# Gate and up products with the weights as the standing operand

## The chip, the cores and the metric

The kernel runs on one core of one Trainium2 chip. The metric is the device time of one execution in microseconds (us), the median of three runs. Below, PE is TensorE's matmul, PEld its loading of the standing operand ("weight load"), DVE is VectorE, ACT is ScalarE, POOL is GpSimd, SP is the engine that issues most DMAs. A matmul holds one operand still in the array (128 rows by up to 128 columns, loaded by an instruction of its own, LDWEIGHTS) and lets the other pass, up to 512 columns; the result goes to PSUM, which has 8 banks of 512 fp32 numbers per partition.

## The reference, cut to what matters

2048 tokens of width 1024 go through a mixing layer and then a mixture of experts: 32 experts of hidden width 512, every token to two of them. The part that the change touches, for the tokens `xblk` of expert `e`:

```python
hdn = jax.nn.silu(xblk @ w_gate[e]) * (xblk @ w_up[e])   # (tokens, 1024) @ (1024, 512), twice
return hdn @ w_down[e]                                    # (tokens, 512) @ (512, 1024)
```

The result is weighted by the router's share and added to the token's row. All is fp32.

## The kernel before

The first 1550 us or so (norm, projections, retention, RWKV, output product, routing) are not touched. Then comes the expert loop, and a final norm.

Products are made in the fp32r format, with each operand split into a high part (rounded by ACT) and a low part (the rest, subtracted by DVE). One product is then three passes into the same PSUM bank: high x high, low x high, high x low. `split_ps` (L171) makes such a pair from a PSUM bank.

The experts are put in an order by load: those at even places (`more(e)`, L43) get 128 + 64 rows of tokens, those at odd places 128. The loop runs over 96 stages (`stages`, L918): (e, 0) gate, (e, 1) up, (e, 2) down, in the order (e, 0), (e, 1), (e-1, 2), so that the down product of one expert comes after the up product of the next. A stage takes four weight chunks of 128 x 1024. They are loaded by SP eight chunks ahead and split by `splits` (L931) on ACT and DVE; six chunks are split before the loop starts. ACT, DVE, PE and POOL run the loop in the order in which it is written.

In a gate or up stage (`mms`, L1061) a 128 x 128 block of the turned tokens `xT` stands and 512 weight columns pass: 8 chunks of the contraction x 3 passes = 24. The result has tokens on partitions. The 64 further rows of an even expert are done by `mms64` and `pair` (L1044, L1081), one stage late in `rest` (L1158): high and low part of the 64 rows stand side by side as 128 columns, so 16 passes of 512 columns do; the two halves of the result are then added by `rows64` (L1090). `gate` applies SiLU, `hidden` multiplies (L1101, L1110).

The down product contracts over the hidden width, so the hidden tile has to have that on partitions: `hidden_turn` (L1121) transposes it on PE, four blocks of 128 x 128 (L1125) or four of 64 rows (`turn64`, L1033), into PSUM, and splits it from there. The tokens themselves are fetched by POOL (`gather`, L1012) and turned by PE in `turn` (L1018, the 128 rows, in the up stage of the expert before) and `turn1` (L1037, the 64 rows, after the second half of the down stage before it).

PSUM: three rotating banks `accr`, three `AL` for the 64-row results, two `tp` for transposes.

Of the kernel before, what the change touches and what calls it, by code (L numbers as in the profile page):

```python
# [9 lines left out]
F32 = mybir.dt.float32  # L10
# [122 lines left out]
def build(tc, A, out, dbg=None, phases=3):  # L133
# [562 lines left out]
    if True:  # L696
# [189 lines left out]
        hlp = lp("hlp", HB)  # L886
        xbp, hdp, htp, yop, xtp, tmp = gp("xbp", 1), gp("hdp", 1), gp("htp", 2), gp("yop", 2), gp("xtp", 2), gp("tmp", TB)
        xbs = [xbp.tile([128 - 64 * i, D], F32, name=f"xb{i}") for i in range(2)]
        hd1 = xbp.tile([64, 512], F32, name="hd1")
        for t in (*xbs, hd1):  # L890
            GP.memset(t, 0.0)

        RAW, LD, LAST, EX = [], [], [], {}
# [123 lines left out]

        def turn(e, hf):  # L1018
            if hf == 0:
                XT[0, e] = xtp.tile([128, 2, 8, 128], F32R, name="xT0", bufs=2)  # L1020
            xT = XT[0, e]
            ps = tp().rearrange("p (k t) -> p k t", k=4)
            hs = slice(hf * 4, hf * 4 + 4)
            for k in range(4):
                PE.transpose(ps[:, k], xbs[0][:, (hf * 4 + k) * 128:(hf * 4 + k + 1) * 128], ident)  # L1025
            split_ps(ps, xT[:, 0, hs], xT[:, 1, hs])

        def turn64(src, n, nm, pool, **kw):

            xT = pool.tile([128, n, 128], F32R, name=nm, **kw)  # L1030
            ps = tp().rearrange("p (k t) -> p k t", t=64)[:, 0:n]
            for k in range(n):
                PE.transpose(ps[:, k], src[:, k * 128:(k + 1) * 128], ident[0:64, 0:64])  # L1033
            split_ps(ps, xT[:, :, 0:64], xT[:, :, 64:128])
            return xT

        def turn1(e):  # L1037
            XT[1, e] = turn64(xbs[1], 8, "xT1", xtp, bufs=1)
            if more(e + 2):
                gather(1, e + 2)  # L1040

# [10 lines left out]
                if k:  # L1052
                    mm(ps, lhs[:, k], wa, False, k == nk - 1)

        def w_in(hl, k):
            return (hl[k // 2][:, z, (k % 2) * 512:(k % 2 + 1) * 512] for z in range(2))

        def w_dn(n):
            return lambda hl, k: (hl[k][:, z, n * 512:(n + 1) * 512] for z in range(2))

        def mms(st, hl, pss, half):  # L1061

            e, w = st
            n = 4 if w < 2 else 2
            for k in range(half * n, half * n + n):
                first, last = k == 0, k == 2 * n - 1
                if w < 2:
                    wa, wb = w_in(hl, k)
                    xT = XT[0, e]
                    mm(pss[0], xT[:, 0, k], wa, first, False)  # L1070
                    mm(pss[0], xT[:, 1, k], wa, False, False)
                    mm(pss[0], xT[:, 0, k], wb, False, last)
                else:
                    hT = HT[2 * e]
                    for n_ in range(2):
                        wa, wb = w_dn(n_)(hl, k)
                        mm(pss[n_], hT[:, 0, k], wa, first, False)
                        mm(pss[n_], hT[:, 1, k], wa, False, False)
                        mm(pss[n_], hT[:, 0, k], wb, False, last)

        def mms64(st, hl, pss):  # L1081

            e, w = st
            if w < 2:
                pair(pss[0], XT[1, e], hl, w_in, 8)
            else:
                for n in range(2):
                    pair(pss[n], HT[2 * e + 1], hl, w_dn(n), 4)

        def rows64(ps, dst, w=None):  # L1090
            t = tmp.tile([64, 512], F32, name="lo64")
            SC.copy(t, ps[64:128])
            if w is None:
                V.tensor_tensor(dst, ps[0:64], t, op=ALU.add)
            else:
                V.tensor_tensor(t, ps[0:64], t, op=ALU.add)
                SC.activation(dst, t, AF.Copy, scale=w)

        GT = {}

        def gate(e, b):  # L1101
            pg = PS.pop((2 * e + b, 0))[0]
            if b == 0:
                GT[e] = hdp.tile([128, 512], F32, name="hd0")
                SC.activation(GT[e], pg, AF.Silu)
            else:
                rows64(pg, hd1)
                SC.activation(hd1, hd1, AF.Silu)

        def hidden(e, b):  # L1110
            pu = PS.pop((2 * e + b, 1))[0]
            if b == 0:
                hd = GT.pop(e)
                V.tensor_tensor(hd, hd, pu, op=ALU.mult)
                HD.append((2 * e, hd))
            else:
                up = tmp.tile([64, 512], F32, name="up")
                rows64(pu, up)
                V.tensor_tensor(hd1, hd1, up, op=ALU.mult)

        def hidden_turn(i, hd):  # L1121
            if i % 2 == 0:
                ps = tp().rearrange("p (k t) -> p k t", k=4)
                for k in range(4):
                    PE.transpose(ps[:, k], hd[:, k * 128:(k + 1) * 128], ident)  # L1125
                HT[i] = htp.tile([128, 2, 4, 128], F32R, name="hT0")
                split_ps(ps, HT[i][:, 0], HT[i][:, 1])
            else:
                HT[i] = turn64(hd, 4, "hT1", htp)

        def result(e, b):
            pn = PS.pop((2 * e + b, 2))
            yo = yop.tile([64 if b else 128, D], F32, name=f"yo{b}", bufs=YB[b])
            for n in range(2):
                o, w = yo[:, n * 512:(n + 1) * 512], ws[b][:, e:e + 1]
                if b:
                    rows64(pn[n], o, w)
                else:
                    SC.activation(o, pn[n], AF.Copy, scale=w)  # L1139
            HT.pop(2 * e + b)  # L1140
            return yo
# [16 lines left out]
        def rest(st, hl):  # L1158

            e, w = st  # L1160
            if not more(e):
                return
            pz_ = PS[2 * e + 1, w]
            mms64(st, hl, pz_)
            r = (gate, hidden, result)[w](e, 1)
            if w == 1:
                HD.append((2 * e + 1, hd1))
            if w == 2:
                ADD.append((SI[0] + ADL[1], 1, e, r))

        mk("moe")
        g0 = gather(0, 0)
# [10 lines left out]
        with tc.manual_schedule(engines=MS):  # L1183
# [4 lines left out]
            for si, st in enumerate(stages):  # L1188
                SI[0] = si
                e, w = st  # L1190
                if si:
                    evict(stages[si - 1])
                if si == len(stages) - 4:
                    gfb = k2.tile([128, D], F32, name="gfb", tag="g2b")
                    SC.dma_start(gfb, A["gf"].broadcast_to([128, D]))
                hl = CH.pop(si)
                nps = 2 if w == 2 else 1
                PS[(2 * e, w)] = [accr.tile([128, 512], F32, name="acc") for _ in range(nps)]
                if more(e):
                    PS[(2 * e + 1, w)] = [AL[(na + i) % 3] for i in range(nps)]  # L1200
                    na += nps
                n0, n1, n2 = NSP[w]
                n0 += si < NXS
                splits(min(n0, SB))
                if si:
                    rest(stages[si - 1], HLP)
                HLP = hl
                splits(n0 - min(n0, SB))
                adds(si)
                for half in range(2):  # L1210
                    mms(st, hl, PS[(2 * e, w)], half)
                    if w == 1 and e + 1 < 32:
                        turn(e + 1, half)
                    elif w == 2 and half and more(e + 2):
                        turn1(e + 2)
                    elif HD and (w == 0 or si == len(stages) - 2):
                        hidden_turn(*HD.pop(0))
                    splits(n1 if half == 0 else n2)
                if w == 1 and e + 2 < 32:
                    gather(0, e + 2)  # L1220
# [7 lines left out]
        with tc.If(nov > 0):  # L1228
            with tc.For_i(0, 32, 1) as e:
                nb = nc.values_load(cni[0:1, 0, bass.ds(e, 1)], min_val=0, max_val=15)  # L1230
                s0 = nc.values_load(cni[0:1, 1, bass.ds(e, 1)], min_val=0, max_val=31 * TS + 192)
                with tc.For_i(0, nb, 1) as j:
                    tc_ = s2.tile([128, 2], F32, name="tc_")
                    for z, d in enumerate((tab_d, tw_d)):
# [4 lines left out]
                    GP.indirect_dma_start(out=xb, out_offset=None, in_=xt_d,  # L1239
                                          in_offset=bass.IndirectOffsetOnAxis(ap=to, axis=0),  # L1240
                                          bounds_check=S - 1, oob_is_err=False)
                    xT = xtp.tile([128, 8, 128], F32, name="xT1", bufs=1)
                    for hf in range(2):
                        ps = tp().rearrange("p (k t) -> p k t", k=4)
                        for k in range(4):
# [2 lines left out]
                    pgu = [accr.tile([128, 512], F32, name="acc") for _ in range(2)]  # L1248
                    for m, wn in enumerate(("wg", "wu")):
                        for k in range(8):  # L1250
                            w = xtp.tile([128, 2, 8, 128], F32, name="xT0").rearrange("p z k t -> p (z k t)")[:, 0:512]
                            SY.dma_start(w, A[wn][bass.ds(e, 1), k // 2, :, (k % 2) * 512:(k % 2 + 1) * 512]
                                         .rearrange("o p c -> (o p) c"))
                            mm(pgu[m], xT[:, k], w, k == 0, k == 7)
                    hd = hdp.tile([128, 512], F32, name="hd0")
                    SC.activation(hd, pgu[0], AF.Silu)
                    V.tensor_tensor(hd, hd, pgu[1], op=ALU.mult)
                    ps = tp().rearrange("p (k t) -> p k t", k=4)
# [3 lines left out]
                    V.tensor_copy(hT, ps)  # L1262
                    py_ = AL[0:2]
                    for k in range(4):
                        w = xtp.tile([128, 2, 8, 128], F32, name="xT0").rearrange("p z k t -> p (z k t)")[:, 0:D]
                        SY.dma_start(w, A["wd"][bass.ds(e, 1), k].rearrange("o p c -> (o p) c"))
                        for n in range(2):
                            mm(py_[n], hT[:, k], w[:, n * 512:(n + 1) * 512], k == 0, k == 3)
# [72 lines left out]
```

## Time and profile before

| | us |
|---|---|
| median of 3 runs (2396.13 to 2401.98) | 2398.52 |
| the profiled execution | 2402.56 |
| its span, first to last instruction | 2400.8 |
| PE busy in the span | 2196.5 |
| expert loop, first to last weight load on PE | about 1560 to 2344 |

In the profile a line such as "L152 PE MATMUL acc<-hl,xT 128\*128 128x512" is a matmul from line 152 (the helper `mm`) into the tile `acc`, with `hl` passing and `xT` standing, 128 rows by 128 columns of the standing operand, and 512 columns passing. The profile calls both fp32 and fp32r operands of matmuls f32. A plain fp32 matmul leaves two records, an fp32r one leaves one. Ends of matmuls are modelled; starts are recorded.

### The profile page before, as it was taken

To read this page: it belongs to the slowest core of one execution; us is meant where nothing else is said; L and a number is where in the kernel's file an instruction comes from. 1 tells how busy PE (TensorE), PEld (TensorE's weight loads), DVE (VectorE), ACT (ScalarE), POOL (GpSimd) and SP (SyncE) were. 2 spreads that over 40 slices of the span, in tenths; PEclk is the share of its full clock that TensorE was granted. 3 is DMA by queue.
4 is the path that set the end of the run, shared out by engine and by line. 5 is a ranking of instruction groups with operands and counts; after the bars stand their busy time and mean duration, and the time that the engine had idled before them with its cause. 6 is when DMAs were issued, how large, how long until landed. Compare 5 with 4: busy or idle time off the path is not lost. (4 is left out here: it accounts for less than half of the span.)

```text
span 2400.8 us, 36373 instructions
## 1 busy us (share of the span) xinstructions
PE 2196.5 (91%) x11816; PEld 1803.3 (75%) x11817; DVE 1698.5 (71%) x3594; ACT 1157.2 (48%) x1963; POOL 779.1 (32%) x1405
## 2 busy tenths in 40 slices
PE   5999889998998989999879999599999999999990
PEld 4887678887777877788768888577777777777770
DVE  4477775878766787667775665767777777777775
ACT  4353443434434344343332232267777677776763
POOL 2036444354531575146541433411112111111110
PEclk9999899999999999999969999799999999999995
DMA  6643254433544325433234445289999999999978
GB/s 212 211 148 99 82 172 135 135 94 99 173 142 122 98 88 167 125 101 99 84 96 130 127 163 175 94 304 306 307 321 299 304 300 320 310 293 303 310 233 297
DMA packets 291298, 454.78 MB, mean 189 GB/s; under 512 B 93392, under 2 KB 164496, under 8 KB 291088
## 3 DMA queue, kind: packets, MB, share of 16 engines
q1 hardware_dynamic: 277136, 414.10, 51.7%
q0 software_dynamic: 13824, 37.80, 7.0%
q8 instruction: 94, 1.54, 0.3%
q14 instruction: 100, 0.82, 0.1%
q10 hardware_dynamic: 144, 0.52, 0.1%
HBM read 375.18 MB, written 81.85 MB: 190 GB/s over the span
## 5 line engine op out<-in xcount | busy, mean ns | idle before, releaser
L152 PE MATMUL pj<-nT,whl 128*128 128x512 f32 x2496 | 628.1, 403 | 9.2 <-DVE nT L319 5.2
L152 PEld LDWEIGHTS pj<-nT,whl 128*128 128x128 f32 x2496 | 466.3, 192 | 107.0 <-DVE nT L319 5.7
L914 DVE TENSOR_TENSOR hl<-raw,hl 128x1024 fp32r<-128x1024 f32 x384 | 448.5, 1219 | 121.5 <-ACT hl L913 121.5
L152 PE MATMUL acc<-hl,xT 128*128 128x512 f32 (+1 forms) x2048 | 508.1, 400 | 0.0
L152 PEld LDWEIGHTS acc<-hl,xT 128*128 128x128 f32 (+1 forms) x2048 | 365.0, 182 | 100.0 <-ACT xT L172 0.2
L913 ACT CAST hl<-raw 128x1024 fp32r<-128x1024 f32 x384 | 378.4, 1048 | 6.7 <-PE tp L152 3.0
L249 ACT CAST whl<-wraw 128x512 fp32r<-128x512 f32 x248 | 152.5, 618 | 299.3 <-PE pj L152 236.1
L250 DVE TENSOR_TENSOR whl<-wraw,whl 128x512 fp32r<-128x512 f32 x248 | 188.0, 761 | 144.2 <-ACT whl L249 138.1
L152 PE MATMUL acc<-hl,hT 128*128 128x512 f32 (+1 forms) x1024 | 249.5, 398 | 0.0
L152 PEld LDWEIGHTS acc<-hl,hT 128*128 128x128 f32 (+1 forms) x1024 | 183.1, 181 | 51.8
L486 POOL TENSOR_TENSOR tm<-xl,ln 128x60 f32<-128x60 f32 (+24 forms) x496 | 173.8, 350 | 105.2 <-DMA ln<-nl_d 60.4
L488 POOL TENSOR_TENSOR xl<-xl,tm 128x60 f32<-128x60 f32 (+24 forms) x496 | 195.3, 394 | 36.6
L152 PE MATMUL acc<-wo,mT 128*128 128x512 f32 x768 | 192.3, 402 | 0.0
L1147 POOL DMA_INDIRECT h_d<-yo,ti x48 | 80.1, 1670 | 299.3 <-ACT yo L1139 180.1
L1014 POOL DMA_INDIRECT xb<-xt_d,ti x48 | 49.5, 1031 | 369.6 <-PE tp L1025 288.0
L152 PEld LDWEIGHTS acc<-wo,mT 128*128 128x128 f32 x768 | 142.3, 191 | 28.7 <-DVE mT L169 0.2
L152 PE MATMUL pj<-whl,nT 128*128 128x256 f32 x768 | 114.3, 298 | 0.3 <-DVE gs L600 0.2
L464 DVE TENSOR_TENSOR pt<-pb,cst 64x512 f32<-64x512 f32 x128 | 88.0, 687 | 22.6 <-PE pb L152 20.8
L152 PEld LDWEIGHTS pj<-whl,nT 128*128 128x128 f32 x768 | 101.6, 199 | 3.0 <-DVE gs L600 0.5
L499 POOL COPY mbd<-pt 32x128 f32<-32x128 f32 x64 | 20.7, 323 | 222.9 <-DVE pt L464 199.1
L172 ACT CAST xT<-tp 128x512 fp32r<-128x512 f32 x80 | 47.0, 588 | 82.6 <-PE tp L1025 54.4
L152 PE MATMUL pb<-ar,bk 64*128 64x128 f32 x512 | 76.3, 295 | 5.2 <-DVE pt L464 3.7
(445 smaller groups left out, 3184.5 us busy)
## 6 DMA issues: line engine op xcount, KB each, us to landing
raw<-in_wg_dram SPq DMA_DIRECT2D x128, 512.0 KB
raw<-in_wu_dram SPq DMA_DIRECT2D x128, 512.0 KB
raw<-in_wd_dram SPq DMA_DIRECT2D x128, 512.0 KB
wraw<-in_win_dram SPq DMA_DIRECT2D x208, 256.0 KB
tr<-pf_d SPq DMA_DIRECT2D x80, 256.0 KB
pf_d<-ev SPq DMA_DIRECT2D x52, 256.0 KB
x<-in_xt_dram SPq DMA_DIRECT2D x32, 256.0 KB
pf_d<-x SPq DMA_DIRECT2D x32, 256.0 KB
```

The source lines that it names most:

```text
L152: PE.matmul(o, l, r, start=start, stop=stop)
L172: SC.copy(dst_h, ps)
L249: SC.copy(hl[:, 0], raw)
L250: V.tensor_tensor(hl[:, 1], raw, hl[:, 0].bitcast(F32), op=ALU.subtract)
L464: V.tensor_tensor(pt[zs, i:i + 2, :, z ^ h], psp[h][zs].rearrange("p (f c) x -> p f c x", f=2), maskp[zs, None, None, :].to_broadcast([64, ...
L486: GP.tensor_tensor(tv, xl[:, 0:r, t:t + 1].to_broadcast([128, r, n]), ln[:, t:t + 1, t + 1:32].to_broadcast([128, r, n]), op=ALU.mult)
L488: GP.tensor_tensor(xl[:, 0:r, t + 1:32], xl[:, 0:r, t + 1:32], tv, op=ALU.add)
L499: GP.tensor_copy(mbd[i * 32:(i + 1) * 32, :, i * 32:(i + 1) * 32], pt[i % 2 * 64:i % 2 * 64 + 32, :, i // 2, 0, 32:64])
L913: (SC.copy if hi is SC else hi.tensor_copy)(hl[:, 0], raw)
L914: lo.tensor_tensor(hl[:, 1], raw, hl[:, 0].bitcast(F32), op=ALU.subtract)
L1014: return GP.indirect_dma_start(out=xbs[b], out_offset=None, in_=xt_d, in_offset=bass.IndirectOffsetOnAxis(ap=ti[b][:, e:e + 1], axis=0), b ...
L1147: GP.indirect_dma_start(out=h_d, out_offset=bass.IndirectOffsetOnAxis(ap=idx, axis=0), in_=y, in_offset=None, bounds_check=S + 127, comput ...
```

## The change

In gate and up stages the operands change places: a 128 x 128 block of weights stands, and all rows of the expert, 128 or 192, pass. The result has the hidden width on partitions, in four blocks of 128, which is how the down product needs it. So `hidden_turn`, `turn64`, the 64-row products of gate and up and their folding go; `hidden_split` splits the hidden tile where it lies in SBUF. The tokens of an even expert stand in one tile of 192 columns, and the 64-row transposes move from the second to the first half of the down stage. For an even expert the four blocks take two PSUM banks (two blocks of 192 columns each), for an odd one a single bank. The down product is as before.

```diff
         def turn(e, hf):
             if hf == 0:
-                XT[0, e] = xtp.tile([128, 2, 8, 128], F32R, name="xT0", bufs=2)
+                XT[e] = xtp.tile([128, 2, 8, 192], F32R, name="xT0")
...
         def turn1(e):
-            XT[1, e] = turn64(xbs[1], 8, "xT1", xtp, bufs=1)
+            ps = tp().rearrange("p (k t) -> p k t", t=64)
+            for k in range(8):
+                PE.transpose(ps[:, k], xbs[1][:, k * 128:(k + 1) * 128], ident[0:64, 0:64])
+            split_ps(ps, XT[e][:, 0, :, 128:192], XT[e][:, 1, :, 128:192])
...
                 if w < 2:
-                    wa, wb = w_in(hl, k)
-                    xT = XT[0, e]
-                    mm(pss[0], xT[:, 0, k], wa, first, False)
-                    mm(pss[0], xT[:, 1, k], wa, False, False)
-                    mm(pss[0], xT[:, 0, k], wb, False, last)
+                    vs = blocks(e, pss)
+                    nj = 4 // len(vs)
+                    for i, (zw, zx) in enumerate(((0, 0), (0, 1), (1, 0))):
+                        for j in range(4):
+                            mm(vs[j // nj][:, j % nj], hl[k // 2][:, zw, (k % 2) * 512 + j * 128:(k % 2) * 512 + j * 128 + 128],
+                               XT[e][:, zx, k, 0:rows(e)], first and i == 0 and j % nj == 0,
+                               last and i == 2 and j % nj == nj - 1)
...
+        def rows(e):
+            return 192 if more(e) else 128
+
+        def blocks(e, pss):
+
+            return [p[:, 0:4 // len(pss) * rows(e)].rearrange("p (j t) -> p j t", t=rows(e)) for p in pss]
+
+        def gate(e, _b):
+            GT[e] = hdp.tile([128, 4, 192], F32, name="hd0")
+            vs = blocks(e, PS.pop((e, 0)))
+            nj = 4 // len(vs)
+            for i, v in enumerate(vs):
+                SC.activation(GT[e][:, i * nj:i * nj + nj, 0:rows(e)], v, AF.Silu)
...
+        def hidden_split(e, hd):
+
+            h = HT[2 * e] = htp.tile([128, 2, 4, 128], F32R, name="hT0")
+            split_ps(hd[:, :, 0:128], h[:, 0], h[:, 1])
+            if more(e):
+                h = HT[2 * e + 1] = htp.tile([128, 4, 128], F32R, name="hT1")
+                split_ps(hd[:, :, 128:192], h[:, :, 0:64], h[:, :, 64:128])
...
         def rest(st, hl):
 
             e, w = st
-            if not more(e):
-                return
-            pz_ = PS[2 * e + 1, w]
-            mms64(st, hl, pz_)
-            r = (gate, hidden, result)[w](e, 1)
-            if w == 1:
-                HD.append((2 * e + 1, hd1))
-            if w == 2:
-                ADD.append((SI[0] + ADL[1], 1, e, r))
+            if w == 2 and more(e):
+                mms64(st, hl, PS[e, 3])
+                ADD.append((SI[0] + ADL[1], 1, e, result(e, 1)))
...
-                    mms(st, hl, PS[(2 * e, w)], half)
+                    mms(st, hl, PS[e, w], half)
                     if w == 1 and e + 1 < 32:
                         turn(e + 1, half)
-                    elif w == 2 and half and more(e + 2):
+                    elif w == 2 and half == 0 and more(e + 2):
                         turn1(e + 2)
-                    elif HD and (w == 0 or si == len(stages) - 2):
-                        hidden_turn(*HD.pop(0))
+                    if half == 0 and HD:
+                        hidden_split(*HD.pop(0))
```

A path for experts with more rows than 128 or 192 (after the loop) is adapted to the tiles' new shapes; no instruction of it runs in the profile.

## Rows read from the trace of the kernel before

**Rows 1.** The page: engines, and the span in 40 slices (tenths).

```profile
PE 2196.5 (91%) x11816; PEld 1803.3 (75%) x11817; DVE 1698.5 (71%) x3594; ACT 1157.2 (48%) x1963; POOL 779.1 (32%) x1405
...
PE   5999889998998989999879999599999999999990
...
DMA  6643254433544325433234445289999999999978
```

**Rows 2.** Stretches: length, busy PE, PEld, DVE, ACT, POOL; granted clock, DMA share, GB/s.

```profile
1600.00:2300.00 700.00, 700.00 (x3269) 542.19 (x3268) 529.87 (x558) 501.08 (x646) 117.54 (x86) 1.00 0.92 306
1428.00:1431.50 3.50, 3.50 (x34) 3.50 (x34) 3.00 (x5) 1.86 (x4) 1.22 (x1) 1.00 1.02 397
264.00:267.00 3.00, 3.00 (x9) 2.52 (x10) 2.60 (x6) 0.00 (x0) 0.00 (x0) 0.50 0.44 86
```

**Rows 3.** Loader in order of time, expert loop: start, length to last end, instruction, count.

```profile
1635.65 0.59 PEld L1125 LDWEIGHTS tp<-ct,hd 128*128 128x128 f32 x4
1636.21 2.63 PEld L152 LDWEIGHTS acc<-hl,xT 128*128 128x128 f32 x12
1639.21 0.32 PEld L1033 LDWEIGHTS tp<-ct,hd 64*128 64x128 f32 x4 [0.37 <-issue]
1639.60 2.63 PEld L152 LDWEIGHTS acc<-hl,xT 128*128 128x128 f32 x12
...
1651.86 0.57 PEld L1033 LDWEIGHTS tp<-ct,xb 64*128 64x128 f32 x8 [0.37 <-DVE hl L914]
...
1659.47 9.18 PEld L152 LDWEIGHTS acc<-hl,xT 128*128 128x128 f32 x40
...
1688.06 0.32 PEld L1033 LDWEIGHTS tp<-ct,hd 64*128 64x128 f32 x4 [0.37 <-issue]
```

**Rows 4.** Loads of the gate and up products, 1600 to 2300 us: busy, mean ns.

```profile
L152 PEld LDWEIGHTS acc<-hl,xT 128*128 128x128 f32 x1598 | 295.0, 188 | 77.2
```

**Rows 5.** Counts over the loop: gate and up passes, transposes of the hidden tile.

```profile
L152 PE MATMUL acc<-hl,xT 128*128 128x512 f32 (+1 forms) x2048 | 508.1, 400 | 0.0
...
L1125 PE MATMUL tp<-ct,hd 128*128 128x128 f32 x128 | 19.2, 272 | 0.0
...
L1033 PE MATMUL tp<-ct,hd 64*128 64x64 f32 x64 | 7.3, 234 | 0.0
```

**Rows 6.** Earlier stages, in order of time, and the mean ns of the same forms.

```profile
133.70 6.01 PE L152 MATMUL pj<-whl,nT 128*128 128x256 f32 x48
...
L152 PE MATMUL pj<-whl,nT 128*128 128x256 f32 x768 | 114.3, 298 | 0.3 <-DVE gs L600 0.2
...
1428.58 2.78 PEld L152 LDWEIGHTS tp<-wrt,xh 128*128 128x128 f32 x24
1428.69 2.79 PE L152 MATMUL tp<-wrt,xh 128*128 128x36 f32 x24
...
L152 PEld LDWEIGHTS tp<-wrt,xh 128*128 128x128 f32 x256 | 32.8, 198 | 0.9
...
230.65 0.54 PEld L152 LDWEIGHTS psr<-uv,pt 64*64 64x64 f32 x8
```

**Rows 7.** Two fp32r loads behind a transpose, 1577.1 to 1577.3 us.

```profile
1577.15 0.30 PEld L152 LDWEIGHTS acc<-hl,xT 128*128 128x128 f32 x2
```

**Rows 8.** Loop: waits (us in total, times, longest), then ACT and DVE pieces.

```profile
DVE hl L914 <- ACT hl L913: 109.1, 72, 1.8
...
PEld tp L1033 <- DVE hl L914: 5.5, 15, 0.4
...
L914 DVE TENSOR_TENSOR hl<-raw,hl 128x1024 fp32r<-128x1024 f32 x344 | 401.7, 1219 | 109.1 <-ACT hl L913 109.1
...
L173 DVE TENSOR_TENSOR xT<-tp,xT 128x512 fp32r<-128x512 f32 x71 | 48.9, 689 | 9.3 <-ACT xT L172 8.5 <-issue 0.6
...
L1114 DVE TENSOR_TENSOR hd<-hd,acc 128x512 f32<-128x512 f32 x28 | 19.0, 677 | 0.0
...
L1108 ACT ACTIVATE hd<-hd 64x512 f32<-64x512 f32 x14 | 8.9, 632 | 10.5 <-DVE hd L1094 9.7 <-issue 0.8
...
L173 DVE TENSOR_TENSOR hT<-tp,hT 128x256 fp32r<-128x256 f32 x14 | 5.9, 425 | 0.0
```

**Rows 9.** A plain fp32 matmul of 512 columns: its first record alone, then both.

```profile
141.11 0.59 PE L152 MATMUL pb<-tr,cst 128*128 128x512 f32 x1
...
141.11 1.02 PE L152 MATMUL pb<-tr,cst 128*128 128x512 f32 x2
```

More of the change, by code (lines that the diff above doesn't have):

```diff
@@ L888, in build @@
         xbs = [xbp.tile([128 - 64 * i, D], F32, name=f"xb{i}") for i in range(2)]
-        hd1 = xbp.tile([64, 512], F32, name="hd1")
-        for t in (*xbs, hd1):
+        for t in xbs:
             GP.memset(t, 0.0)
@@ L1025, in turn @@
                 PE.transpose(ps[:, k], xbs[0][:, (hf * 4 + k) * 128:(hf * 4 + k + 1) * 128], ident)
[L1026 to L1035, printed above, removed]
+            split_ps(ps, XT[e][:, 0, hs, 0:128], XT[e][:, 1, hs, 0:128])
         def turn1(e):
-            XT[1, e] = turn64(xbs[1], 8, "xT1", xtp, bufs=1)
+            ps = tp().rearrange("p (k t) -> p k t", t=64)
+            for k in range(8):
+                PE.transpose(ps[:, k], xbs[1][:, k * 128:(k + 1) * 128], ident[0:64, 0:64])
+            split_ps(ps, XT[e][:, 0, :, 128:192], XT[e][:, 1, :, 128:192])
             if more(e + 2):
@@ L1053, in pair @@
                     mm(ps, lhs[:, k], wa, False, k == nk - 1)
-        def w_in(hl, k):
-            return (hl[k // 2][:, z, (k % 2) * 512:(k % 2 + 1) * 512] for z in range(2))
         def w_dn(n):
@@ L1067, in mms @@
                 if w < 2:
-                    wa, wb = w_in(hl, k)
-                    xT = XT[0, e]
-                    mm(pss[0], xT[:, 0, k], wa, first, False)
-                    mm(pss[0], xT[:, 1, k], wa, False, False)
-                    mm(pss[0], xT[:, 0, k], wb, False, last)
+                    vs = blocks(e, pss)
[5 more added lines that the diff above has]
+                               last and i == 2 and j % nj == nj - 1)
                 else:
@@ L1081, in mms64, with rows64 @@
         def mms64(st, hl, pss):
[L1083 to L1090, printed above, removed]
+            for n in range(2):
+                pair(pss[n], HT[2 * st[0] + 1], hl, w_dn(n), 4)
+        def rows64(ps, dst, w):
             t = tmp.tile([64, 512], F32, name="lo64")
             SC.copy(t, ps[64:128])
[L1093 to L1097, printed above, removed]
@@ L1099, in build @@
-        GT = {}
[L1101 to L1129, printed above, removed]
+            V.tensor_tensor(t, ps[0:64], t, op=ALU.add)
+            SC.activation(dst, t, AF.Copy, scale=w)
@@ new lines, in hidden @@
+        def hidden(e, _b):
+            hd = GT.pop(e)
+            vs = blocks(e, PS.pop((e, 1)))
+            nj = 4 // len(vs)
+            for i, v in enumerate(vs):
+                o = hd[:, i * nj:i * nj + nj, 0:rows(e)]
+                V.tensor_tensor(o, o, v, op=ALU.mult)
+            HD.append((e, hd))
+        def hidden_split(e, hd):
[4 more added lines that the diff above has]
+                split_ps(hd[:, :, 128:192], h[:, :, 0:64], h[:, :, 64:128])
@@ L1131, in result @@
         def result(e, b):
-            pn = PS.pop((2 * e + b, 2))
+            pn = PS.pop((e, 2 + b))
             yo = yop.tile([64 if b else 128, D], F32, name=f"yo{b}", bufs=YB[b])
@@ L1197, in build @@
                 nps = 2 if w == 2 else 1
-                PS[(2 * e, w)] = [accr.tile([128, 512], F32, name="acc") for _ in range(nps)]
+                PS[e, w] = [accr.tile([128, 512], F32, name="acc") for _ in range(nps)]
                 if more(e):
-                    PS[(2 * e + 1, w)] = [AL[(na + i) % 3] for i in range(nps)]
+                    ps = [AL[(na + i) % 3] for i in range(nps)]
                     na += nps
+                    if w < 2:
+                        PS[e, w] += ps
+                    else:
+                        PS[e, 3] = ps
                 n0, n1, n2 = NSP[w]
@@ L1241, in build @@
                                           bounds_check=S - 1, oob_is_err=False)
-                    xT = xtp.tile([128, 8, 128], F32, name="xT1", bufs=1)
+                    xT = hlp.tile([128, 2, D], F32, name="hl")[:, 0].rearrange("p (k t) -> p k t", k=8)
                     for hf in range(2):
@@ L1250, in build @@
                         for k in range(8):
-                            w = xtp.tile([128, 2, 8, 128], F32, name="xT0").rearrange("p z k t -> p (z k t)")[:, 0:512]
+                            w = hlp.tile([128, 2, D], F32, name="hl")[:, 0, 0:512]
                             SY.dma_start(w, A[wn][bass.ds(e, 1), k // 2, :, (k % 2) * 512:(k % 2 + 1) * 512]
@@ L1254, in build @@
                             mm(pgu[m], xT[:, k], w, k == 0, k == 7)
-                    hd = hdp.tile([128, 512], F32, name="hd0")
+                    hd = hdp.tile([128, 4, 192], F32, name="hd0").rearrange("p k t -> p (k t)")[:, 0:512]
                     SC.activation(hd, pgu[0], AF.Silu)
@@ L1264, in build @@
                     for k in range(4):
-                        w = xtp.tile([128, 2, 8, 128], F32, name="xT0").rearrange("p z k t -> p (z k t)")[:, 0:D]
+                        w = hlp.tile([128, 2, D], F32, name="hl")[:, 0]
                         SY.dma_start(w, A["wd"][bass.ds(e, 1), k].rearrange("o p c -> (o p) c"))
```

## The prediction

> **What bounds the kernel now.** I read the page first: TensorE is busy nearly throughout, and from slice 26 on the DMA engines are too [rows 1]. That late stretch is the expert loop, where the whole change lies, so I asked for the busy time of each engine between 1600 and 2300 us [rows 2]: PE 700 of 700 us at the full clock (2.4 GHz), its weight loader 542, DVE 530, ACT 501, DMA engines 0.92. A busy PE alone proves little, as matmul ends are modelled. So I read the loader in order of time [rows 3]: loads follow one another with next to no idle time, and the pattern of two experts returns after 1688.06 - 1639.21 = 48.85 us; 16 times that is 781.6 us, the whole loop. In the list of waits DVE waits 109.1 us for ACT's casts, while PE's loader waits for DVE only 15 times, 0.4 us at the longest [rows 8]. DMA at 0.92 is close behind, but weights are fetched ahead and PE is not seen waiting for them. So TensorE's passes set the loop's time, and a change here is worth what it changes in the sum of passes.
>
> What one pass costs must be taken from starts, not from durations. Forty loads in a row take 9.18 us, the last of them 0.188 [rows 3, 4]: (9.18 - 0.188) / 39 = 230.6 ns per pass of 512 columns. Its own load, 188 ns, lies behind the 512 columns of the pass before.
>
> **The change: passes.** Before, the tokens stand and 512 weight columns pass: for one projection of one expert 24 passes, and 16 more for the 64 further rows of an even expert; 32 x 2 x 24 + 16 x 2 x 16 = 2048 in all, the count of [rows 5]. They cost 2048 x 230.6 ns = 472.3 us. After, 128 x 128 blocks of weights stand and the 128 (odd experts) or 192 (even) token columns pass: 8 k-chunks x 4 blocks x 3 products (high x high, high x low, low x high) = 96 passes for every projection whether even or odd, 32 x 2 x 96 = 6144, each with a load of its own. Counted by passing columns that is fair: 96 x 192 = 18432 against 40 x 512 = 20480 (even), 96 x 128 = 12288 against 24 x 512 = 12288 (odd). But the trace has to say what a pass costs whose columns take less time than its load.
>
> It shows no pass in this number format (fp32r) under 256 columns, so I bound it. From above by the nearest in format: 48 passes of 256 columns take 6.01 us, the last 0.298: (6.01 - 0.298) / 47 = 121.5 ns [rows 6]. From the side of the load: 24 loads of 128 columns in plain fp32, with only 36 columns passing at a time, take 2.78 us, the last 0.198: (2.78 - 0.198) / 23 = 112.3 ns [rows 6]. There the columns cannot be what takes the time; the load is. Eight loads of 64 columns take 0.54 us [rows 6], at most 67 ns each, so a load goes by its columns. And for the format here two loads stand directly behind each other, 0.30 us for two of 0.19: 110 ns apart [rows 7]. So fp32r loads are not quicker than fp32 ones. I read it as: the next load starts as soon as the pass before it starts, one load ahead and no more; a pass costs the longer of its columns and the load, and below 256 columns the load is the longer. Of 112.3 and 121.5 I take 115 ns for 192 and for 128 columns alike: nearer the lower, since there too the load binds, with a little of the 256-column row's surplus, whose cause I can't see. 6144 x 115 ns = 706.6 us; the ends give 690.0 and 746.5.
>
> On the load the Trainium skill speaks against this reading: "TensorE: Matmul & The Clock Gate", section "Weight-path perf modes", has a fast weight load that is on for 128 weights when the input is not FP32. If fp32r counted as not FP32 there, loads would vanish behind even 128 columns, and the sum would go by columns (a rival below). The pair 110 ns apart [rows 7] says it does not count.
>
> **The change: the rest.** Gate x up now comes out with the hidden dimension on partitions, so its transposes go. Four of 128 x 128 and their way back to the products take 1636.21 - 1635.65 = 0.56 us, 32 times 17.9; four of 64 rows 1639.60 - 1639.21 = 0.39, 16 times 6.2 [rows 3, 5]: 24.1 us off PE. (The loader's 0.37 us idle before the latter I count at nothing: a 512-column pass still streams there.) The transposes of the gathered tokens stay, as do the 1024 passes of the down product.
>
> On ACT and DVE the folding of the 64-row results goes (two copies, two adds, one SiLU and one product per even expert), and a split of the hidden tile from SBUF replaces the one from PSUM; even experts' SiLU and product become two instructions of 384 columns. By [rows 8] these are pieces of 0.4 to 0.7 us; per two experts DVE has 24 x 1.219 = 29.3 us of splits and some 8 us of the rest, in a period that grows to about 61. All this stays under PE; cost nothing. Were it uncovered, the worst place is the even expert's 64-row transpose, now half a stage earlier and needed by the very next stage's first pass instead of one stage later. Queued ahead of its subtraction on DVE are one product (0.68) and four splits (4 x 1.22), then its own 0.69: ready 6.2 us into the stage. PE gets there after 24 passes, the transposes (0.57 [rows 3]) and the 16 passes of the 64-row down product: 40 x 0.2306 + 0.57 = 9.8 us. So 3.6 us of cover; without it at most the 0.6 + 0.69 of its split would show, 16 times: 20 us.
>
> Gathers on POOL are issued at the same points or half a stage sooner, and have a period of slack. SP's weight loads are asked for by the splits, so they come at the slower pace: their demand drops from 306 to about 306 x 48.85 / 62 = 241 GB/s. The first stage must now wait for both gathers and the 64-row split before its first pass: about 2 us, once.
>
> **Sum.** 706.6 - 472.3 - 24.1 + 2 = +212 us. The profiled execution took 2402.6 us (span 2400.8), 4.0 above the median of 2398.5; so 2402.6 + 212 = 2615 on its scale, 2611 for the median. With the ends: 2594 to 2651.
>
> **Rivals.**
> *Columns bind, not loads (no change).* If a load can be brought forward by more than one pass, or is quick in this format, a pass costs by its columns. From the 512- and 256-column rows: (230.6 - 121.5) / 256 = 0.426 ns per column and 12.4 ns fixed, so 94.2 ns at 192 and 66.9 at 128; 3072 x (94.2 + 66.9) = 494.9 us, and 494.9 - 472.3 - 24.1 + 2 = 0: 2399, not slower. It decides as soon as a load costs under 67 ns. For it: nothing but that no narrow fp32r pass stands in the trace. Against it: 112.3 ns with 36 columns, and 110 between two fp32r loads [rows 6, 7]. The Trainium skill's fast weight load would lead here. 4 in 100.
>
> *Narrow passes run at half rate.* A plain fp32 pass of 512 columns takes 1.02 - 0.59 = 0.43 us [rows 9], 0.84 ns per column. If fp32r reaches its double rate only with wide passes, 192 columns take 161 ns, and 128 stay at the load's 115: 3072 x 276 = 847.9, sum +353, 2752. For it: no run here shows a narrower fp32r pass. Against it: 256 columns still run at 121.5. 8 in 100.
>
> *Full fall back to fp32:* each product then is two such passes (two records, as in [rows 9]): 1695.7 us, 3600. 6 in 100.
>
> *The clock falls.* If the granted clock falls to 0.50, the 1.2 GHz level that [rows 2] has at 264 us, in the gate and up stages of odd experts, their 3072 passes of 115 ns take twice that, 353 us more: 2964. Against it: the stretch at 1428 us, load-bound all along with 36 columns, kept 1.00 [rows 2]. 3 in 100.
>
> *A late operand* (the 64-row split above): 2611 + 20 = 2631. 3 in 100.
>
> **How the numbers follow.** Load-bound 76, late operand 3, half rate 8, fall back 6, clock 3, columns 4. The forecast is the first, 2611, its own range 2594 to 2651. The stated range reaches from a little below its lower end to the half-rate case, 2580 to 2765, which leaves about 13 in 100 out. Half of the column case's chance falls within 0.3% of before, a fair line for what can be told from no change here, and half on the faster side: faster 0.02, same 0.02, slower 0.96.
>
> **What would show it.** Right: 6144 loads and passes in the expert loop at 110 to 122 ns from start to start, the same for 192 and 128 columns; the loader busy without a gap; a period of two experts near 61 us; DMA share near 0.72; no transposes out of the hidden tile; clock at 1.00. Wrong: steps of 67 and 94 ns (columns), of 160 ns in even experts only (half rate), twice as many records (fall back), a granted clock of 0.50, or a weight load waiting for DVE at the start of even experts' gate stages.

## The result, and the profile after

The changed kernel takes 2588.9 us (median of 4, 2583.2 to 2593.8) against 2400.3 for the kernel before in the same runs: ratio 1.0786, 95% interval 1.0756 to 1.0815, slower by 188.7 us. Forecast were 2611 us and +212; the stated range, 2580 to 2765, holds the result, but the range of the load-bound case itself, 2594 to 2651, is missed by 5 us at its lower end.

The expert loop, busy times and granted clock as in [rows 2]:

```profile
1600.00:2500.00 900.00, 900.00 (x7038) 844.60 (x7038) 527.26 (x554) 502.31 (x645) 123.14 (x88) 1.00 0.78 247
```

PE is busy throughout as before and the clock is at its upper level, but the loader is now busy for 844.60 of 900 us where it was for 542 of 700, and DMA's share fell from 0.92 to 0.78. The load has become what PE is busy with. From the page, with busy, mean ns and idle time before, to set beside [rows 5]:

```profile
L152 PE MATMUL acc<-xT,hl 128*128 128x192 f32 (+1 forms) x6144 | 700.6, 275 | 1.7 <-ACT xT L172 1.5
L152 PEld LDWEIGHTS acc<-xT,hl 128*128 128x128 f32 x6144 | 696.8, 193 | 4.9 <-ACT xT L172 1.7
```

The loader in order of time, over the period of two experts that [rows 3] shows for before (start, length, instruction, count):

```profile
1645.09 5.44 PEld L152 LDWEIGHTS acc<-hl,hT 128*128 128x128 f32 x24
1650.57 16.27 PEld L152 LDWEIGHTS acc<-xT,hl 128*128 128x128 f32 x144
1666.79 0.42 PEld L1023 LDWEIGHTS tp<-ct,xb 128*128 128x128 f32 x4
1667.18 5.44 PEld L152 LDWEIGHTS acc<-xT,hl 128*128 128x128 f32 x48
...
1675.97 0.57 PEld L1029 LDWEIGHTS tp<-ct,xb 64*128 64x128 f32 x8 [0.37 <-issue]
...
1683.02 16.28 PEld L152 LDWEIGHTS acc<-xT,hl 128*128 128x128 f32 x144
...
1736.29 0.57 PEld L1029 LDWEIGHTS tp<-ct,xb 64*128 64x128 f32 x8 [0.37 <-issue]
```

The matmuls that belong to its two rows of 144 loads, with the columns that pass (128 and 192):

```profile
1650.80 16.19 PE L152 MATMUL acc<-xT,hl 128*128 128x128 f32 x144
...
1683.25 16.22 PE L152 MATMUL acc<-xT,hl 128*128 128x192 f32 x144
```

The rows to compare are the two of 144 loads. At 1650.57 stand the stages of an odd expert (128 columns pass), at 1683.02 those of an even one (192): 16.27 and 16.28 us, (16.27 - 0.19) / 143 = 112.4 ns per pass in both. Half as many columns again cost nothing. The period is 1736.29 - 1675.97 = 60.32 us, where before had 48.85; 16 times the difference of 11.47 is 183.5 us. The rest, some 5 us, fits the loop's first stage:

```profile
1564.14 0.93 PEld L152 LDWEIGHTS acc<-xT,hl 128*128 128x128 f32 x4 [1.73 <-ACT xT L172]
1565.51 18.73 PEld L152 LDWEIGHTS acc<-xT,hl 128*128 128x128 f32 x140 [0.44 <-DVE xT L173]
```

It waits for the 64-row split, 1.73 and 0.44 us, and begins at the lower clock (granted 0.50 from 1560 to 1568 us): 140 loads in 18.73 us is more than the 15.7 that 112.4 ns each would make. The kernel before begins in the same way, with waits of 0.22 and 0.44 us and a few slow passes, so only the difference counts. That it makes up the 5 us is an account and no measurement.

### The profile page after: what moved, and what is told of

Same layout as the page of the kernel before. It is cut to its first block, busy times and chain, and to the rows that moved or that the text cites. A ratio compares the mean times of both kernels' runs of the same rounds, so it can differ in the third digit from the quotient of the medians.

```text
span 2588.0 us, 43977 instructions
## 1 busy us (share of the span) xinstructions
PE 2376.6 (92%) x15720; PEld 2101.9 (81%) x15721; DVE 1665.8 (64%) x3562; ACT 1134.3 (44%) x1931; POOL 785.7 (30%) x1404
## 5 line engine op out<-in xcount | busy, mean ns | idle before, releaser
L152 PE MATMUL acc<-xT,hl 128*128 128x192 f32 (+1 forms) x6144 | 700.6, 275 | 1.7 <-ACT xT L172 1.5
L152 PEld LDWEIGHTS acc<-xT,hl 128*128 128x128 f32 x6144 | 696.8, 193 | 4.9 <-ACT xT L172 1.7
L173 DVE TENSOR_TENSOR xT<-tp,xT 128x512 fp32r<-128x512 f32 x80 | 55.1, 689 | 164.2 <-ACT xT L172 164.2
L1098 ACT ACTIVATE hd<-acc 128x384 f32<-128x384 f32 (+1 forms) x48 | 23.5, 525 | 185.2 <-PE acc L152 185.2
```

Source lines behind the costliest of these rows:

```text
L152: PE.matmul(o, l, r, start=start, stop=stop)
L173: V.tensor_tensor(dst_l, ps, dst_h.bitcast(F32), op=ALU.subtract)
```

## The experiments

Four kernels, told as differences from the changed kernel, and one built on the fourth, with the question whether the load alone sets the 112 ns, and what would have to be done about it.

**Half the load (e1).** All but the first and last four passes of a stage become two passes with 64 weight columns standing; both write the lower 64 hidden rows.

```diff
-                            mm(vs[j // nj][:, j % nj], hl[k // 2][:, zw, (k % 2) * 512 + j * 128:(k % 2) * 512 + j * 128 + 128],
-                               XT[e][:, zx, k, 0:rows(e)], first and i == 0 and j % nj == 0,
-                               last and i == 2 and j % nj == nj - 1)
+                            f_ = (first and i == 0) or (last and i == 2)
+                            for q in range(1 if f_ else 2):
+                                m, o = 128 if f_ else 64, (k % 2) * 512 + j * 128 + q * 64
+                                mm(vs[j // nj][0:m, j % nj], hl[k // 2][:, zw, o:o + m], XT[e][:, zx, k, 0:rows(e)],
+                                   first and i == 0 and j % nj == 0, last and i == 2 and j % nj == nj - 1)
```

> The changed kernel with 88 of the 96 gate and up passes of a stage each replaced by two passes that load 64 weight columns instead of 128 (the first and the last four stay). Both halves are written to the lower 64 hidden rows, so the hidden tile is not the reference's; the same token columns pass, twice as often: 5632 passes become 11264. Load theory (a pass costs the longer of its load and its columns, and 128 columns of load are the longer): with half the load the columns bind, 94 ns at 192 and 67 ns at 128, so 2 x 2816 x (94.2 + 66.9) = 907 us against 632 us, +275: 2864 us, with even and odd stages apart for the first time. Rival, a fixed cost of some 112 ns per load and pass whatever its size: twice 632 us, 3221 us, even and odd alike.

Measured: 2790.7 us, 73 under the load theory's 2864. The fixed cost per pass (3221) is out. Its loader in the second half of an even and of an odd up stage (88 half loads and 4 full ones), and the transposes that follow each:

```profile
1653.17 8.37 PEld L152 LDWEIGHTS acc<-xT,hl 128*64 128x64 f32 x92
1661.49 0.43 PEld L1023 LDWEIGHTS tp<-ct,xb 128*128 128x128 f32 x4
...
1685.07 5.86 PEld L152 LDWEIGHTS acc<-xT,hl 128*64 128x64 f32 x92
1690.87 0.42 PEld L1023 LDWEIGHTS tp<-ct,xb 128*128 128x128 f32 x4
```

Start to start this is 8.32 and 5.80 us; less four full ones at 0.112, over 88: 89 ns at 192 columns and 61 ns at 128. Even and odd now differ: with half the load, 192 columns bind. At 128 columns this run can't tell what binds, for loads of 64 columns stand (0.54 - 0.14) / 7 = 58 ns apart in [rows 6], and 61 is as near to that as to the columns. Both prices are 5 to 6 ns under my line (94.2 and 66.9), and over 11264 passes that is some 62 of the 73 us: what stands above the bare columns is smaller here than in the passes of 256 and 512 columns, from which the line was drawn. Two half loads with their passes, 122 to 178 ns, are dearer than a full one, so this is no way to mend the change.

**Fewer columns (e2).** The same passes and loads, 64 columns each.

```diff
         def rows(e):
-            return 192 if more(e) else 128
+            return 64
...
-            split_ps(hd[:, :, 0:128], h[:, 0], h[:, 1])
+            hb = hd[:, :, None, 0:64].to_broadcast([128, 4, 2, 64])
+            split_ps(hb, *(h[:, z].rearrange("p k (z t) -> p k z t", z=2) for z in range(2)))
...
-                split_ps(hd[:, :, 128:192], h[:, :, 0:64], h[:, :, 64:128])
+                split_ps(hd[:, :, 0:64], h[:, :, 0:64], h[:, :, 64:128])
```

> The changed kernel with only 64 token columns passing in every gate and up pass (the other tokens' hidden values are copies of these, so the output is not the reference's); loads and the number of passes as before. Load theory: nothing changes on PE, 112 ns a pass, 2589 us within 10. Rival, the columns have a part in the 112 ns (as they would by the line through the 256- and 512-column rows, 0.426 ns each): 64 columns at 40 ns, 6144 x 72 ns less, 2145 us; a mixture would lie between.

Measured: 3142.5 us; neither. Three stretches of it (columns as above): most of a gate and up pair, the down stage and the beginning of the next pair, and the rest of that pair.

```profile
1664.00:1697.00 33.00, 33.00 (x151) 32.42 (x152) 7.03 (x9) 7.24 (x10) 2.03 (x2) 0.50 0.36 107
1699.00:1705.00 6.00, 6.00 (x42) 5.41 (x40) 3.98 (x5) 4.34 (x8) 1.58 (x1) 1.00 0.93 305
1706.00:1743.00 37.00, 37.00 (x172) 36.61 (x172) 8.76 (x10) 6.97 (x10) 1.08 (x1) 0.50 0.37 127
```

PE is busy without a gap and its loader for 32.42 of 33 us, yet the granted clock is 0.50 (1.2 GHz) while most of the narrow passes run; it comes back to 1.00 around the 512-column passes of the down stage and falls again a few microseconds into the next gate stage. The loader shows the price at either level:

```profile
1701.79 1.31 PEld L152 LDWEIGHTS acc<-xT,hl 128*128 128x128 f32 x10
...
1702.02 3.09 PEld L152 LDWEIGHTS acc<-xT,hl 128*128 128x128 f32 x27
...
1730.05 10.43 PE L152 MATMUL acc<-xT,hl 128*128 128x64 f32 x48
```

At the upper clock ten loads take 1.31 us, the last some 0.19: 124 ns with a slower first step behind a 512-column pass. From the second load on (the next row, which runs on to 1705 us) it is (3.09 - 0.19) / 26 = 112. At the lower clock 48 passes take 10.43 us, about 213 ns each, nearly twice 112. So per pass the load theory holds (64 columns cost no less than 192), and the load's time goes with TensorE's clock; the expectation failed because I held the clock for given. What brings the clock down here, no run isolates. A falling clock was a rival of the prediction at 3 in 100. In the changed kernel's loop it did not come true, in this one it did.

**One load for two results (e3).** In odd experts' stages the high weight block stands once while high and low part of the rows pass together, 256 columns.

```diff
+                            if not more(e):
+                                v = pss[j // 2].rearrange("p (j z t) -> p j z t", j=2, z=2)[:, j % 2]
+                                if i == 0:
+                                    mm(v, lw_, XT[e][:, :, k, 0:128], first and j % 2 == 0, False)
+                                elif i == 2:
+                                    mm(v[:, 0], lw_, XT[e][:, 0, k, 0:128], False, last and j % 2 == 1)
+                                continue
...
+        def fold(p):
+            v = p.rearrange("p (j z t) -> p j z t", j=2, z=2)
+            t = tmp.tile([128, 2, 128], F32, name="lo128", bufs=2)
+            SC.copy(t, v[:, :, 1])
+            V.tensor_tensor(t, t, v[:, :, 0], op=ALU.add)
+            return t
```

> The changed kernel, but in gate and up stages of odd experts the high weight block is loaded once and the high and the low part of the 128 rows pass together as 256 columns; the two results are added on ACT and DVE when they leave PSUM. 64 passes in place of 96. Load theory: 32 at 121.5 and 32 at 112.3 ns, 7.48 us a stage against 10.78, 32 stages: -106 us, 2483 us. Rival, the adding on ACT and DVE (two copies, two adds more at the start of each following stage) becomes the new wait: up to 1.5 us a stage back, 2531 us. Second rival, the time goes by columns: 12288 columns as before, no change, 2589 us.

Measured: 2477.8 us (2477.0 to 2479.9), ratio to before 1.0341 (1.0311 to 1.0371). Set against the kernel before in its own runs this is +81 us where the changed kernel has +189, so 107 us less, forecast were 106; the same 12288 columns pass in fewer, wider passes. The loader's 96 loads of the odd stages:

```profile
1639.28 11.29 PEld L152 LDWEIGHTS acc<-xT,hl 128*128 128x128 f32 x96
```

(11.29 - 0.19) / 95 = 116.8 ns a load, the mean of 121.5 and 112 that was expected. The adding on ACT and DVE cost nothing on PE.

**Where the loss sits (e4).** Even experts turned round, odd ones as in the kernel before.

```diff
+                if w < 2 and not more(e):
+                    wa, wb = (hl[k // 2][:, z, (k % 2) * 512:(k % 2 + 1) * 512] for z in range(2))
+                    mm(pss[0], XT[e][:, 0, k, 0:128], wa, first, False)
+                    mm(pss[0], XT[e][:, 1, k, 0:128], wa, False, False)
+                    mm(pss[0], XT[e][:, 0, k, 0:128], wb, False, last)
...
+            if not more(e):
+                ps = tp().rearrange("p (k t) -> p k t", k=4)
+                hf = hd.rearrange("p k t -> p (k t)")
+                for k in range(4):
+                    PE.transpose(ps[:, k], hf[:, k * 128:(k + 1) * 128], ident)
+                return split_ps(ps, h[:, 0], h[:, 1])
```

> Even experts (192 rows) as in the changed kernel, odd experts (128 rows) as in the kernel before, with their hidden transposes. Load theory: of the 188 us lost, odd experts' stages lost 96 x 112.3 - 24 x 230.6 = 5.25 us each (32 times, 168, less the transposes) and even ones 96 x 112.3 - 40 x 230.6 = 1.56 us each (32 times, 50, less some 17 to 20 of transposes): +31 us against the kernel before, 2431 us. Rival, the loss is spread over both kinds (the new order, the wider tile, the splits from SBUF): half of it, 2494 us.

Measured: 2430.9 us (2425.6 to 2437.6), ratio to before 1.0135 (1.0103 to 1.0168), +34 us. So some 154 of the 189 us belong to odd experts, where 24 passes of 512 columns had become 96 narrow ones.

**High and low rows of even experts over one load (e6).** What e1 to e4 say together: keep odd experts as they were; for even ones put high and low rows, 384 columns, over one load of the high block.

```diff
+            if w < 2 and more(e):
+                for k in range(8):
+                    for j in (2 * half, 2 * half + 1):
+                        v = pss[j][:, 0:384].rearrange("p (z t) -> p z t", z=2)
+                        wh_, wl_ = (hl[k // 2][:, z, (k % 2) * 512 + j * 128:(k % 2) * 512 + j * 128 + 128] for z in range(2))
+                        mm(v, wh_, XT[e][:, :, k], k == 0, False)
+                        mm(v[:, 0], wl_, XT[e][:, 0, k], False, k == 7)
+                return
...
+                v = PS[e, w][j][:, 0:384].rearrange("p (z t) -> p z t", z=2)
+                t = tmp.tile([128, 192], F32, name="lo192", bufs=2)
+                SC.copy(t, v[:, 1])
+                V.tensor_tensor(t, t, v[:, 0], op=ALU.add)
```

> Built on the mixed kernel (even experts turned round, odd ones as in the kernel before): in gate and up stages of even experts the high weight block is loaded once and the high and low parts of the 192 rows pass together as 384 columns, into four PSUM banks of which two are emptied at half time; high and low results are added on ACT and DVE. 64 passes in place of 96. Load theory: a 384-column pass hides the next load, 0.426 x 384 + 12.4 = 176 ns (with the 7 ns of surplus that the half loads showed, 171), a 192-column pass still costs the load's 112: 32 x (171 to 176 + 112) = 9.1 to 9.2 us a stage against 40 x 230.6 = 9.22 in the kernel before, whose hidden transposes of even experts (about 1 us) and part of the wait around the token transposes go as well: 2376 us, 15 to 25 under the kernel before, and some 55 under the mixed kernel. Rival, ACT and DVE, which get four copies and four adds more per stage in a period as short as before, bind: the gain is lost again, 2400 us or more.

Measured: 2383.2 us (2380.7 to 2384.6), ratio to before 0.9941 (0.9926 to 0.9956): 14 us or 0.6% faster than the kernel before, clear of the noise but small, and 7 short of the forecast.

```profile
1651.03 0.57 PEld L1029 LDWEIGHTS tp<-ct,xb 64*128 64x128 f32 x8 [0.37 <-issue]
...
1658.51 13.91 PEld L152 LDWEIGHTS acc<-xT,hl 128*128 128x128 f32 x96
...
1698.48 0.57 PEld L1029 LDWEIGHTS tp<-ct,xb 64*128 64x128 f32 x8 [0.36 <-issue]
...
1600.00:2300.00 700.00, 699.79 (x3967) 612.14 (x3966) 563.07 (x697) 526.56 (x785) 119.82 (x87) 1.00 0.93 314
```

The 96 loads take 13.91 us, 144 ns each, the mean of 176 and 112. A stage's 64 passes thus cost 9.24 us, no less than the 9.22 of the kernel before: the passes break even, and most of the gain is what the hidden transposes of even experts had cost. The period is 1698.48 - 1651.03 = 47.45 us against 48.85, 16 times 1.40 = 22 us, as expected; 14 to 18 of it arrive (14 in the medians, 18 between the two profiled spans). What is missing between the spans lies mostly at the loop's two ends:

```profile
1566.78 16.01 PEld L152 LDWEIGHTS acc<-xT,hl 128*128 128x128 f32 x96 [2.97 <-DVE xT L173]
...
2315.39 0.42 PEld L1148 LDWEIGHTS tp<-ct,hd 128*128 128x128 f32 x4 [1.11 <-DVE hd L1138]
```

The first stage waits 2.97 us for the 64-row split (the kernel before 0.44 at most), its 96 loads take 16.01 us in place of 13.91, as the clock is still at its lower level when they begin, and the last hidden tile comes 1.11 us late. In between ACT and DVE do not bind: PE is busy for 699.79 of 700 us, and in the list of waits from 1600 to 2300 us its loader waits for DVE once, 0.6 us.

## Why the prediction was right

**The bound** was read rightly: TensorE's passes set the loop before, and they set it after; no other engine or queue took over.

**The price of a pass** was the step that decided. With the two bounds of 112.3 and 121.5 ns I took 115; measured were 112.4, so the lower bound, a plain fp32 load with 36 columns passing [rows 6], was not only nearer but the price itself. The surplus that I feared from the 256-column row is one of wide passes (e1, and e3 where the 256-column passes keep it). That a load goes by its columns was right, but the row named for it doesn't show it: its loads of 64 columns have 64 rows too, and the loads of the 64-row transposes in [rows 3], 128 columns wide, stand (0.57 - 0.14) / 7 = 61 ns apart. It is e1, with 128 rows and 64 columns, that shows it for a product. 6144 x 112.4 = 690.6 us; some 35 passes at the lower clock at the loop's start add about 3.5, together 694 instead of 706.6: 12 us of the 23 that I forecast too much.

**What I held unchanged, the transposes of the tokens, became cheaper** by the count from load to load in which I made the forecast, and that is most of the other half; without it the result would not have fallen below 2594. Before, a set of four and the load behind it stand so:

```profile
1642.27 0.59 PEld L1025 LDWEIGHTS tp<-ct,xb 128*128 128x128 f32 x4
1642.83 2.63 PEld L152 LDWEIGHTS acc<-hl,xT 128*128 128x128 f32 x12
```

Four transposes of 128 x 128 with their way back took 1642.83 - 1642.27 = 0.56 us, and 1667.18 - 1666.79 = 0.39 after. All of it lies in the first step, from the first load of the four to the second: 0.23 us before, 0.06 after; the other steps are 0.11 in both. That first load starts while the pass ahead of it still runs, and that pass now lasts 112 ns instead of 231. So the transposes themselves are no quicker: the count had charged them with the end of a wide pass. 64 times 0.17 is 11 us. The hidden tile's own transposes went as counted. So the sum that the traces give is 694 - 472.3 - 24.1 - 11 + 2 = +189, the measured difference. It closes to a microsecond or two, not better, since the kernel before has about 1 us of slow passes at its loop's start as well, and the pause before the 64-row hidden transposes, which I counted at nothing, held the next matmul up by about 0.1 us, 16 times.

**What lies beside PE** stayed there. The late operand did not come: in the list of waits of the changed kernel between 1600 and 2500 us PE's loader has one entry only, for its own issue:

```profile
PEld tp L1029 <- issue: 5.5, 15, 0.4
```

In [rows 8] 15 pauses before the same transposes, of the same length, are put down to DVE. Here the list finds nothing that they wait for, so that entry was probably no wait for DVE.

The first stage's wait (2 us forecast) is the 1.73 + 0.44 above. DMA came out at 0.78 and 247 GB/s where I had 0.72 and 241.

**The rivals.** Columns instead of loads: out, by the two equal rows of 144 and by e3, where the same columns cost 107 us less. Half rate and fall back to fp32: out, 192 columns cost 112 ns and not 160, and each product leaves one record. The clock: out for this change, but closer than 3 in 100 suggests, as e2 shows. On the load the Trainium skill's page "TensorE: Matmul & The Clock Gate", section "Weight-path perf modes", has a fast load for inputs that are not FP32; the trace shows 112.4 ns for 128 columns of fp32r, the same as for plain fp32, so no fast load shows here for fp32r.

## What to carry to other kernels

Before turning a product round, count loads as well as columns: in fp32r a pass of 64, 128 or 192 columns cost what its 128-column load costs, 112 ns at the upper clock, so an operand that passes 128 columns pays more than twice its columns (53 ns at 2.4 GHz). The price of a pass that the trace doesn't show can be had from another format, if a row there isolates the resource that will bind. Where high and low parts of one operand meet the same standing block, let them pass side by side over one load; that took 107 us off the narrow passes of e3, and in e6 it only drew level with passes of 512 columns.

## What the runs showed that I had not expected

The granted clock was 0.50 in stretches of e2 in which the records leave PE no gap, PE and loader busy for 33.00 and 32.42 of 33 us; the changed kernel's loop had 1.00. The load slows with the clock, 112 to about 213 ns. And what a pass costs above its bare columns at 2.4 GHz (0.417 ns each) is larger in wide passes: 9 ns at 192 columns (89 in e1, with half a load), 15 at 256 and 17 at 512 [rows 3, 6].
